# Attention logits of two pairs of steps in one visit of TensorE

## The chip, the cores and the metric

The kernel runs on one core of a Trainium2 chip. The metric is the device time in microseconds of one execution. Before the change it is 630.37 us (median of 3 runs, 630.08 to 630.44).

## The reference

A decoder trunk of two layers on 256 tokens of width 1024, all in float32. Each layer is

```
h = h + Mixer(RMSNorm(h))
h = h + square(relu(RMSNorm(h) @ w1)) @ w2        # 1024 -> 4096 -> 1024
```

The mixer of layer a is dilated sliding-window attention with three groups of 8 heads (windows and dilations 128/1, 512/4, 2048/16), merged by their softmax denominators; that of layer b is causal attention with 16 heads (with 256 tokens there is one block, its own). Both normalise queries and keys per head of 64, add a relative-position bias per head and mask:

```
q, k = rmsnorm(q_head), rmsnorm(k_head)
p = softmax(q @ k.T / 8 + bias + mask)            # float32, stable
o = p @ v ; Mixer = concat(o) @ w_o
```

## The kernel before, in words

All weights stream from HBM through one sequence of units of 256 rows x 512 columns. ScalarE rounds each 128-row slice to a high half (`next_hi`, L158) and VectorE makes the low half (`next_lo`, L173, instructions of L177 and L179); a dense product is then three matmuls per step (`mm3`, L231 to L233, and L654 to L656 in the MLP). The splits run several slices ahead of TensorE.

The order of the work is written out by hand. Every engine runs its instructions in the order in which the program issues them. After each `mm3` of a projection `beat()` (L211) counts one beat, issues what is due by then (`defer(beats, fn)`, L207; equal due times in the order in which they were deferred), and every second beat one more slice of the splits. So a due time is a place between the dense matmuls of TensorE, and at the same time a place in the queues of the other engines.

Attention is cut into 16 steps a layer, taken in pairs `m` (steps 2m and 2m+1, the two heads of a 128-row pair). In layer a a step is 128 query rows of one head position and four blocks of 128 keys; in layer b it is a whole head, three blocks. For a pair the stages are:

- `logits` (L505): 8 (layer b: 6) small matmuls a step, 16 or 12 a visit, on half the rows of the array each, into two PSUM banks of the tag `s`.
- `softmax` (L522) defers three things: one beat later `biased` (L536, VectorE: add the bias, L537, and take row maxima, L539), three beats later `exps` (L543, ScalarE, L545), five beats later `normed` (L547, VectorE: reciprocal, L550, and scaling, L552). They work in a buffer `L` of the pool, of which there are three.
- `turn` (L558): one step's probabilities are transposed on TensorE (L563) into a bank of the tag `tp`; a beat later ScalarE copies them out (`keep`, L567).
- `weigh` (L570): probabilities times values into a bank of the tag `o`, then `finish` (L587) splits the sums.

In `logits` a step counts matmuls as 4 (or 3) blocks, so a pair's visit has 8 matmuls in layer a and 6 in layer b as program statements, each run as two instructions in the trace (x16, x12).

`place` (L704) gives the due times: `logit_at`, `turn_at` and `weigh_at` per pair, counted from the start of the layer's projection. `project` has 16 beats for each of its entries (9 in layer a, 6 in layer b). Between them also stand the norms of the query and key heads: for an entry that ends at beat e, `head_norm` (L457) has GpSimd's power at e+4, the scaling of the two tiles of heads on VectorE at e+10 and e+11 (`normed`, L467), and their transposes on TensorE at e+13 and e+14 (`turned`, L472), also into banks `tp`, of which there are two. The entries of layer a with heads end at beats 16, 32, 48, 64, 80 and 96.

PSUM has eight banks: two each of `s`, `o`, `tp` and `acc`. The banks `o` hold nothing in a projection until the first `weigh`, due at beat 133 in layer a and 82 in layer b. A bias buffer is loaded for two head pairs ahead, by SP's queue, after the last `biased` of the pair before.

Of the kernel before, what the change touches and what calls it, by code (L numbers as in the profile page):

```python
# [67 lines left out]
def trunk(ctx, tc, x, rel_bias, norm_mix, norm_ffn, a_w_qkv, a_q_gain, a_k_gain, a_w_o,  # L68
          b_w_qkv, b_q_gain, b_k_gain, b_w_o, ffn_w1, ffn_w2, onehot, mask_a, mask_b, out):
    nc = tc.nc  # L70
# [12 lines left out]
    def bank(tag, name):  # L83
        return ps.tile([P, 512], F32, tag=tag, bufs=2, name=name)

    def work(tag, bufs, name):
        return act.tile([P, 512], F32, tag=tag, bufs=bufs, name=name)
# [119 lines left out]
    def defer(beats, fn):  # L207
        st["seq"] += 1
        later.append((st["beat"] + beats, st["seq"], fn))
# [279 lines left out]
    def attend(layer):  # L489


        npair = 4 if layer == "a" else 8
        steps = [(p, a, t) for p in range(npair) for t in range(NT) for a in range(2)] if layer == "a" else \
            [(p, a, None) for p in range(npair) for a in range(2)]
        nst = len(steps) // npair
        bias, probs, turned, o = {}, {}, {}, {}

        def blocks(a, t):

            if layer == "b":  # L500
                return [(1, None, 0), (1, None, 1), (0, None, 0)]
            own = [(t, g, t) for g in range(NG)]
            return own + [(0, 0, 1)] if t == 0 else [(1, 0, 0)] + own

        def logits(first):  # L505

            todo = []
            for n in (first, first + 1):
                p, a, t = steps[n]
                sp = bank("s", f"s_{layer}_{n}")  # L510
                rows = slice(a * HD, (a + 1) * HD)
                c, pr = p // 4, p % 4
                for i, (qt, g, kt) in enumerate(blocks(a, t)):
                    if layer == "a":
                        c, pr = g, p
                    todo.append((i, a, sp[:, i * P:(i + 1) * P], T["q"][rows, c, pr, qt * P:(qt + 1) * P],
                                 T["k"][rows, c, pr, kt * P:(kt + 1) * P]))
                softmax(n, sp)
            for _, _, dst, q, k in sorted(todo, key=lambda e: e[:2]):
                nc.tensor.matmul(dst, lhsT=q, rhs=k, start=True, stop=True)  # L520

        def softmax(n, sp):  # L522
            p, a, t = steps[n]
            L = work("L", 3, f"L_{layer}_{n}")
            bl = blocks(a, t)
            w = len(bl) * P
            nmax = small.tile([P, NT], F32, tag="nmax", name=f"nmax_{layer}_{n}")
            den = small.tile([P, NT], F32, tag="den", name=f"den_{layer}_{n}")
            off = P if layer == "a" and t == 0 else 0
            rows_of = []  # L530
            for qt in range(NT):
                mine = [i for i in range(len(bl)) if bl[i][0] == qt]
                if mine:
                    rows_of.append((qt, L[:, mine[0] * P:(mine[-1] + 1) * P]))

            def biased():  # L536
                nc.vector.tensor_add(L[:, :w], sp[:, :w], bias[p][:, a, off:off + w])  # L537
                for qt, lv in rows_of:
                    nc.vector.tensor_reduce(nmax[:, qt:qt + 1], lv, op=ALU.max, axis=AX.X, negate=True)  # L539
                if n % nst == nst - 1 and p + 2 < npair:  # L540
                    bias[p + 2] = load_bias(layer, p + 2)

            def exps():  # L543
                for qt, lv in rows_of:
                    nc.scalar.activation(lv, lv, AF.Exp, bias=nmax[:, qt:qt + 1], accum_out=den[:, qt:qt + 1])  # L545

            def normed():  # L547
                q0, q1 = rows_of[0][0], rows_of[-1][0]
                d = den[:, min(q0, q1):max(q0, q1) + 1]
                nc.vector.reciprocal(d, d)  # L550
                for qt, lv in rows_of:
                    nc.vector.tensor_scalar(lv, lv, den[:, qt:qt + 1], None, op0=ALU.mult)  # L552
            defer(1, biased)
            defer(3, exps)
            defer(5, normed)
            probs[n] = L

        def turn(n):  # L558
            p, a, t = steps[n]
            w = len(blocks(a, t)) * P  # L560
            tp = bank("tp", f"pt_{layer}_{n}")
            for i in range(w // P):
                nc.tensor.transpose(out=tp[:, i * P:(i + 1) * P], in_=probs[n][:, i * P:(i + 1) * P], identity=rev)  # L563
            pT = turned[n] = work("pT", NPT, f"pT_{layer}_{n}")

            def keep():
                nc.scalar.activation(pT[:, :w], tp[:, :w], AF.Copy)  # L567
            defer(1, keep)

        def weigh(first):  # L570

            todo = []
            for n in (first, first + 1):
                p, a, t = steps[n]
                if n % nst == 0:
                    o[p] = bank("o", f"o_{layer}_{p}")
                bl = blocks(a, t)
                col = ((p % 4) * 2 + a) * HD
                for i, (qt, g, kt) in enumerate(bl):
                    v = V[g if layer == "a" else p // 4]  # L580
                    todo.append((i, a, o[p][a * HD:(a + 1) * HD, qt * P:(qt + 1) * P], v[:, kt, col:col + HD],
                                 turned[n][:, i * P:(i + 1) * P], i == 0 or bl[i - 1][0] != qt,
                                 i == len(bl) - 1 or bl[i + 1][0] != qt))
            for _, _, dst, v, pt, start, stop in sorted(todo, key=lambda e: e[:2]):
                nc.tensor.matmul(dst, lhsT=v, rhs=pt, start=start, stop=stop)  # L585

        def finish(p):  # L587

            if p % 4 == 0:
                oT[p // 4] = tuple(act.tile([P, 4, S], F32R, tag="ol", bufs=4, name=f"o{s}_{layer}_{p}") for s in "hl")  # L590
            hi, lo = (z[:, p % 4, :] for z in oT[p // 4])
            i = o[p][:, 0:S]
            if layer == "b":
                hi, lo = (z.rearrange("p (b t q) -> p t q b", b=2, t=2) for z in (hi, lo))
                i = i.rearrange("p (t q b) -> p t q b", t=2, b=2)
            nc.scalar.activation(hi, i, AF.Copy)
            nc.vector.tensor_sub(lo, i, hi.bitcast(F32))

        def first_bias():
            for p in range(2):  # L600
                bias[p] = load_bias(layer, p)

        return first_bias, logits, turn, weigh, finish

    def wo_group(layer, n, acc, hc, ks, nhc, by_tile=False):
# [96 lines left out]
    defer(16, bias_vectors)  # L702

    def place(layer, logit_at, turn_at, weigh_at):  # L704
        first_bias, logits, turn, weigh, finish = attend(layer)
        nst = 4 if layer == "a" else 2
        defer(30 if layer == "a" else 2, first_bias)
        for n in range(16):
            m = n // 2
            defer(turn_at(m) + n % 2 * 3, lambda n=n: turn(n))  # L710
            if n % 2 == 0:
                defer(logit_at(m), lambda n=n: logits(n))
                defer(weigh_at(m), lambda n=n: weigh(n))
            if n % nst == nst - 1:
                defer(weigh_at(m) + 1, lambda n=n: finish(n // nst))


    place("a", lambda m: 64 + 14 * m if m < 4 else (112, 119, 126, 132.5)[m - 4],
          lambda m: 73 + 14 * m if m < 4 else 120 + 7 * (m - 4),
          lambda m: (133, 133, 133, 133, 146, 146, 150, 150)[m])  # L720
    project("a", order_a)
    acc = {0: [bank("acc", f"wo_a_0_{t}") for t in range(NT)]}
    wo_group("a", 0, acc[0], 0, [0, 1], 1, True)
# [10 lines left out]
    def to_second(n, y):  # L734
        add_half(n, y, rstd)
        norm_half(2, n, natural=True, lead=3)

    ffn(0, to_second)
    place("b", lambda m: 48 + 8 * m if m < 4 else (81.5, 87.5, 94, 100.5)[m - 4],
          lambda m: 57 + 8 * m if m < 4 else 90 + 6 * (m - 4),  # L740
          lambda m: (82, 82, 88, 88, 101, 101, 113, 113)[m])
    project("b", order_b)
    acc = {0: [bank("acc", f"wo_b_0_{t}") for t in range(NT)]}
    wo_group("b", 0, acc[0], 0, range(4), 2, True)
# [49 lines left out]
```

## Time and profile before

| | |
|---|---|
| time, median of 3 runs | 630.37 us |
| profiled execution | 630.4 us |
| its span, first to last instruction | 628.6 us |
| TensorE busy | 623.0 us (99%) |
| VectorE busy | 426.8 us (68%) |
| ScalarE busy | 385.1 us (61%) |
| GpSimd busy | 36.6 us (6%) |
| DMA, mean | 181 GB/s |

The span is split by engine: an engine is busy when an instruction of it runs. TensorE's matmuls are pipelined, so their durations overlap, and the distance from one start to the next says more than a duration. The granted clock of TensorE was full in every stretch of the page. Layer a's projection with its attention fills the first 137 us, layer b's lies between 332 and 417 us; in both stretches VectorE is busy for most of the time, although it is not over the whole span.

### The profile page before, as it was taken

Reading aid. Unit: us, or ns where it says so; the run is one execution under the profiler, and the core shown is the slowest. Engines: PE = TensorE matmul, PEld = TensorE weight load, DVE = VectorE, ACT = ScalarE, POOL = GpSimd, SP = SyncE. Lnnn points to the kernel's source line nnn. Section 1 sums busy time; section 2 is a strip of 40 time slices with the busy share of each in tenths; the row PEclk is TensorE's granted clock in tenths of the full one; section 3 lists DMA queues with packets and bytes.
Section 4 is the critical chain, followed back from the end, with each engine's and each line's share of the span. In section 5 each row is a group of like instructions: output and inputs, shape, how many; then the busy total and the mean of one; then the engine's idle time right before and its main releaser. Section 6 shows DMA issues by size and latency. Waiting matters only on the chain.

```text
span 628.6 us, 10380 instructions
## 1 busy us (share of the span) xinstructions
PE 623.0 (99%) x3902; PEld 541.2 (86%) x3902; DVE 426.8 (68%) x767; ACT 385.1 (61%) x742; POOL 36.6 (6%) x23
## 2 busy tenths in 40 slices
PE   8999999999999999999999999999999999999997
PEld 7778887888989989998988878778998899899886
DVE  5877988856875476467547789887776745754651
ACT  6866876765765356456537868777665644663540
POOL 1222221000000000000000332000000000000000
PEclk9999999999999999999999999999999999999999
DMA  7977456433655563574556657563467446645801
GB/s 250 315 196 241 124 187 174 163 108 124 215 174 190 205 223 140 187 254 140 174 179 202 196 180 195 142 186 125 157 211 260 147 161 230 220 127 191 250 18 68
DMA packets 74539, 113.62 MB, mean 181 GB/s; under 512 B 4585, under 2 KB 30505, under 8 KB 74489
## 3 DMA queue, kind: packets, MB, share of 16 engines
q1 hardware_dynamic: 74312, 112.82, 55.7%
q8 instruction: 31, 0.51, 0.3%
q14 instruction: 20, 0.16, 0.1%
q10 hardware_dynamic: 176, 0.14, 0.1%
HBM read 111.81 MB, written 1.13 MB: 180 GB/s over the span
## 4 chain that ended last, share of the span: by engine, by line
PE 97%; DVE 1%; DMA 1%; ACT 0%; issue 0%; DVEq 0%; SPq 0%; ACTq 0%
PE up L654 10%; PE up L656 9%; PE up L655 9%; PE y L231 9%; PE y L233 9%; PE y L232 9%; PE acc_a L231 6%; PE acc_a L232 5%; PE acc_a L233 5%; PE acc_b L231 3%; PE acc_b L233 3%; PE acc_b L232 3%; PE s_a L520 1%; PE o_a L585 1%; PE ut L355 1%; PE wo_b L231 1%
## 5 line engine op out<-in xcount | busy, mean ns | idle before, releaser
L179 DVE SCALAR_TENSOR_TENSOR lo<-raw,gt,hi 128x512 fp32r<-128x512 f32 x248 | 174.6, 745 | 7.4 <-ACT hi L169 7.2
L169 ACT ACTIVATE hi<-raw,gt 128x512 fp32r<-128x512 f32 x248 | 163.0, 714 | 5.7 <-PE y L233 2.8
L654 PE MATMUL up<-uh,hi 128*128 128x256 f32 x512 | 143.6, 281 | 0.0
L655 PE MATMUL up<-ul,hi 128*128 128x256 f32 x512 | 143.3, 280 | 0.0
L656 PE MATMUL up<-uh,lo 128*128 128x256 f32 x512 | 143.3, 280 | 0.0
L177 DVE TENSOR_TENSOR lo<-raw,hi 128x512 fp32r<-128x512 f32 x152 | 98.0, 685 | 42.0 <-ACT hi L167 41.8
L167 ACT ACTIVATE hi<-raw 128x512 fp32r<-128x512 f32 x152 | 88.1, 624 | 52.6 <-PE up L655 20.2
L231 PE MATMUL y<-hi,hh 128*128 128x512 f32 x256 | 99.8, 390 | 0.0
L233 PE MATMUL y<-hi,hl 128*128 128x512 f32 x256 | 99.6, 389 | 0.0
L232 PE MATMUL y<-lo,hh 128*128 128x512 f32 x256 | 99.6, 389 | 0.0
L656 PEld LDWEIGHTS up<-uh,lo 128*128 128x128 f32 x512 | 97.8, 191 | 0.0
L655 PEld LDWEIGHTS up<-ul,hi 128*128 128x128 f32 x512 | 96.1, 188 | 0.6
L654 PEld LDWEIGHTS up<-uh,hi 128*128 128x128 f32 x512 | 96.1, 188 | 0.5
L640 DVE TENSOR_TENSOR r<-r 128x512 f32<-128x512 f32 (+1 forms) x36 | 22.7, 631 | 65.6 <-ACT r L638 65.6
L638 ACT ACTIVATE r<-up 128x512 f32<-128x512 f32 (+1 forms) x36 | 19.8, 550 | 72.8 <-PE up L656 72.4
L231 PE MATMUL acc_a<-hi,uh 128*128 128x512 f32 x144 | 60.6, 421 | 0.0
L232 PE MATMUL acc_a<-lo,uh 128*128 128x512 f32 x144 | 57.0, 396 | 0.0
L233 PE MATMUL acc_a<-hi,ul 128*128 128x512 f32 x144 | 56.9, 395 | 0.0
L233 PEld LDWEIGHTS y<-hi,hl 128*128 128x128 f32 x256 | 48.0, 188 | 10.0
L231 PEld LDWEIGHTS y<-hi,hh 128*128 128x128 f32 x256 | 48.1, 188 | 9.4
L232 PEld LDWEIGHTS y<-lo,hh 128*128 128x128 f32 x256 | 48.1, 188 | 9.4
L231 PE MATMUL acc_b<-hi,uh 128*128 128x512 f32 x96 | 40.1, 418 | 0.0
(128 smaller groups left out, 777.4 us busy)
## 6 DMA issues: line engine op xcount, KB each, us to landing
raw<-in_ffn_w_dram SPq DMA_DIRECT2D x128, 512.0 KB, 4.9
raw<-in_a_w_qkv_dram SPq DMA_DIRECT2D x64, 256.0 KB, 4.3
raw<-in_b_w_qkv_dram SPq DMA_DIRECT2D x24, 512.0 KB, 4.6
raw<-in_b_w_o_dram SPq DMA_DIRECT2D x8, 512.0 KB, 5.0
bias_a<-vdram_a SPq DMA_DIRECT2D x20, 128.0 KB, 6.0
raw<-in_a_w_qkv_dram SPq DMA_DIRECT2D x4, 512.0 KB, 6.6
raw<-in_a_w_o_dram SPq DMA_DIRECT2D x4, 512.0 KB
bias_b<-vdram_b SPq DMA_DIRECT2D x8, 256.0 KB, 4.5
```

Of the source, the lines that this page charges most:

```text
L167: nc.scalar.activation(hi, w, AF.Copy)
L169: nc.scalar.activation(hi, w, AF.Copy, scale=gt[:, gain + c:gain + c + 1])
L177: nc.vector.tensor_sub(lo, w, hi.bitcast(F32))
L179: nc.vector.scalar_tensor_tensor(lo, w, gt[:, gain + c:gain + c + 1], hi.bitcast(F32), op0=ALU.mult, op1=ALU.subtract)
L231: nc.tensor.matmul(acc, lhsT=a[0], rhs=b[0], start=first, stop=False)
L232: nc.tensor.matmul(acc, lhsT=a[0], rhs=b[1], start=False, stop=False)
L233: nc.tensor.matmul(acc, lhsT=a[1], rhs=b[0], start=False, stop=last)
L638: defer(1, lambda: nc.scalar.activation(r, banks[b][:, :w], AF.Relu))
L640: defer(3, lambda: nc.vector.tensor_mul(r, r, r))
L654: nc.tensor.matmul(o, lhsT=whi[:, cols], rhs=uh, start=k == 0, stop=False)
L655: nc.tensor.matmul(o, lhsT=whi[:, cols], rhs=ul, start=False, stop=False)
L656: nc.tensor.matmul(o, lhsT=wlo[:, cols], rhs=uh, start=False, stop=k == 7)
```

## The change

Pairs get due times in tables. The logits of two neighbouring pairs may now have one due time; then the second pair is computed into the two banks `o` instead of `s`. In layer a this holds for all four twos of pairs, in layer b for the first four pairs. `turn` of the two steps of a pair is 2 beats apart instead of 3. There are four buffers `L` instead of three; the scratch that the program reserves for DMAs issued by GpSimd is cut to 8192 bytes.

```diff
-        def logits(first):
+        def logits(first, tag):
...
-                sp = bank("s", f"s_{layer}_{n}")
+                sp = bank(tag, f"s_{layer}_{n}")
...
-            L = work("L", 3, f"L_{layer}_{n}")
+            L = work("L", 4, f"L_{layer}_{n}")
...
-            defer(turn_at(m) + n % 2 * 3, lambda n=n: turn(n))
+            defer(turn_at[m] + n % 2 * 2, lambda n=n: turn(n))
             if n % 2 == 0:
-                defer(logit_at(m), lambda n=n: logits(n))
-                defer(weigh_at(m), lambda n=n: weigh(n))
+                tag = "o" if m and logit_at[m] == logit_at[m - 1] else "s"
+                defer(logit_at[m], lambda n=n, tag=tag: logits(n, tag))
+                defer(weigh_at[m], lambda n=n: weigh(n))
...
-    place("a", lambda m: 64 + 14 * m if m < 4 else (112, 119, 126, 132.5)[m - 4],
-          lambda m: 73 + 14 * m if m < 4 else 120 + 7 * (m - 4),
-          lambda m: (133, 133, 133, 133, 146, 146, 150, 150)[m])
+    place("a", (64, 64, 84, 84, 112, 112, 126, 126),
+          (73, 77, 93, 97, 121, 125, 135, 139),
+          (133, 133, 133, 133, 146, 146, 150, 150))
...
-    place("b", lambda m: 48 + 8 * m if m < 4 else (81.5, 87.5, 94, 100.5)[m - 4],
-          lambda m: 57 + 8 * m if m < 4 else 90 + 6 * (m - 4),
-          lambda m: (82, 82, 88, 88, 101, 101, 113, 113)[m])
+    place("b", (48, 48, 64, 64, 81.5, 87.5, 94, 100.5),
+          (57, 61, 73, 77, 90, 96, 102, 108),
+          (82, 82, 88, 88, 101, 101, 113, 113))
...
-    nc = _bacc.Bacc("TRN2", target_bir_lowering=False, num_devices=1)
+    nc = _bacc.Bacc("TRN2", target_bir_lowering=False, num_devices=1, dynamic_dma_scratch_size=8192)
```

## Rows read from the trace of the kernel before

**Rows 1.** The page, section 1: busy us (share of the span), instructions.
```profile
PE 623.0 (99%) x3902; PEld 541.2 (86%) x3902; DVE 426.8 (68%) x767; ACT 385.1 (61%) x742; POOL 36.6 (6%) x23
```

**Rows 2.** All waits of TensorE: waiter, releaser, us, times, longest.
```profile
PE warm_ps L261 <- DVE idle L255: 1.1, 1, 1.1
PE ut L355 <- DMA h<-in_x_dram: 0.6, 1, 0.6
```

**Rows 3.** Timeline of TensorE, layer a's first logits: start, us, operation.
```profile
57.99 0.39 PE L231 MATMUL acc_a<-hi,uh 128*128 128x512 f32 x1
...
58.45 0.39 PE L233 MATMUL acc_a<-hi,ul 128*128 128x512 f32 x1
58.77 1.16 PE L520 MATMUL s_a<-kT_a,qT_a 64*128 64x128 f32 x16
59.86 0.51 PE L231 MATMUL acc_a<-hi,uh 128*128 128x512 f32 x1
60.20 0.40 PE L232 MATMUL acc_a<-lo,uh 128*128 128x512 f32 x1
```

**Rows 4.** Timeline of TensorE, layer b's first logits and first `turn`.
```profile
368.89 0.94 PE L520 MATMUL s_b<-kT_b,qT_b 64*128 64x128 f32 x12
369.76 0.50 PE L231 MATMUL acc_b<-hi,uh 128*128 128x512 f32 x1
...
377.14 0.49 PE L563 MATMUL pt_b<-rev,L_b 128*128 128x128 f32 x3
```

**Rows 5.** TensorE around logits with 64 weighing matmuls, then 32 alone.
```profile
123.03 0.40 PE L233 MATMUL acc_a<-hi,ul 128*128 128x512 f32 x1
...
128.43 0.39 PE L232 MATMUL acc_a<-lo,uh 128*128 128x512 f32 x1
...
138.70 0.40 PE L233 MATMUL wo_a<-hi,ol_a 128*128 128x512 f32 x1
...
141.26 0.40 PE L232 MATMUL wo_a<-lo,oh_a 128*128 128x512 f32 x1
```

**Rows 6.** Timeline of VectorE after layer a's first logits; idle time before in brackets.
```profile
59.96 0.69 DVE L537 TENSOR_TENSOR L_a<-s_a,bias_a 128x512 f32<-128x512 f32 x1 [0.87 <-PE s_a L520]
...
62.61 0.74 DVE L179 SCALAR_TENSOR_TENSOR lo<-raw,gt,hi 128x512 fp32r<-128x512 f32 x1
...
64.73 0.16 DVE L550 RECIPROCAL den_a<-den_a 128x1 f32<-128x1 f32 x1
...
65.92 1.41 DVE L179 SCALAR_TENSOR_TENSOR lo<-raw,gt,hi 128x512 fp32r<-128x512 f32 x2
```

**Rows 7.** Timeline of TensorE, layer a's first `turn`.
```profile
66.17 0.60 PE L563 MATMUL pt_a<-rev,L_a 128*128 128x128 f32 x4
```

**Rows 8.** Timeline of VectorE from beat 84 to the scaling of heads.
```profile
78.21 2.07 DVE L179 SCALAR_TENSOR_TENSOR lo<-raw,gt,hi 128x512 fp32r<-128x512 f32 x3
81.75 0.69 DVE L467 TENSOR_TENSOR z_a<-z_a,r_a 128x512 f32<-128x512 f32 x1 [1.47 <-POOL r_a L463]
```

**Rows 9.** Timeline of VectorE after layer b's first logits.
```profile
369.86 0.56 DVE L537 TENSOR_TENSOR L_b<-s_b,bias_b 128x384 f32<-128x384 f32 x1 [0.66 <-PE s_b L520]
...
372.09 0.74 DVE L179 SCALAR_TENSOR_TENSOR lo<-raw,gt,hi 128x512 fp32r<-128x512 f32 x1
...
374.21 0.16 DVE L550 RECIPROCAL den_b<-den_b 128x2 f32<-128x2 f32 x1
...
375.53 0.74 DVE L179 SCALAR_TENSOR_TENSOR lo<-raw,gt,hi 128x512 fp32r<-128x512 f32 x1
```

**Rows 10.** A low half made on VectorE, and its first use on TensorE.
```profile
89.19 0.74 DVE L179 SCALAR_TENSOR_TENSOR lo<-raw,gt,hi 128x512 fp32r<-128x512 f32 x1
...
93.60 0.39 PE L232 MATMUL acc_a<-lo,uh 128*128 128x512 f32 x1
```

**Rows 11.** Groups of ScalarE: shapes, count, busy us, mean ns, idle before.
```profile
L545 ACT ACTIVATE L_a<-L_a,nmax_a 128x512 f32<-128x512 f32 x16 | 11.5, 722 | 7.5 <-DVE nmax_a L539 7.5
L567 ACT ACTIVATE pT_a<-pt_a 128x512 f32<-128x512 f32 x16 | 9.5, 593 | 5.7 <-PE pt_a L563 5.7
```

More of the change, by code (lines that the diff above doesn't have):

```diff
@@ L709, in place @@
             m = n // 2
-            defer(turn_at(m) + n % 2 * 3, lambda n=n: turn(n))
+            defer(turn_at[m] + n % 2 * 2, lambda n=n: turn(n))
             if n % 2 == 0:
-                defer(logit_at(m), lambda n=n: logits(n))
-                defer(weigh_at(m), lambda n=n: weigh(n))
+                tag = "o" if m and logit_at[m] == logit_at[m - 1] else "s"
+                defer(logit_at[m], lambda n=n, tag=tag: logits(n, tag))
+                defer(weigh_at[m], lambda n=n: weigh(n))
             if n % nst == nst - 1:
-                defer(weigh_at(m) + 1, lambda n=n: finish(n // nst))
-    place("a", lambda m: 64 + 14 * m if m < 4 else (112, 119, 126, 132.5)[m - 4],
-          lambda m: 73 + 14 * m if m < 4 else 120 + 7 * (m - 4),
-          lambda m: (133, 133, 133, 133, 146, 146, 150, 150)[m])
+                defer(weigh_at[m] + 1, lambda n=n: finish(n // nst))
+    place("a", (64, 64, 84, 84, 112, 112, 126, 126),
+          (73, 77, 93, 97, 121, 125, 135, 139),
+          (133, 133, 133, 133, 146, 146, 150, 150))
     project("a", order_a)
```

## The prediction

> **What bounds the kernel now.** I read the page's busy table first: TensorE is busy in 623.0 of 628.6 us [rows 1]. Then its waits: the longest is 1.1 us, at the very start [rows 2]. So TensorE never stands still in the middle of the program, and the time is the sum of what it issues. Two things can change that sum: less time per visit of small matmuls, or a wait where there was none. For the first I read TensorE's timeline around such visits, for the second VectorE's timeline in the same stretches, because VectorE makes what TensorE's later visits read.
>
> The profiled execution took 630.4 us (span 628.6, 1.8 around it); the median of the three runs is 630.37, so sums made on the one hold for the other.
>
> **What the change saves.** Two dense matmuls start 0.46 us apart over two steps, 57.99 to 58.45, so a plain step is 0.23 and a beat of three is 0.69 [rows 3]. From the last dense start before a visit of logits (58.45) to the second dense start behind it (60.20) are 1.75 us; two plain steps would be 0.46, so the visit costs 1.29 [rows 3]. From its first matmul to the next dense one a visit of 16 (8 pairs) takes 1.09 us, one of 12 (6 pairs) 0.87 [rows 3, 4]: 0.11 a pair. Of the 1.29, 8 x 0.11 = 0.88 is the pairs and 0.41 is getting in and out. That part is paid once less whenever two visits become one. Layer a goes from eight visits to four, layer b from eight to six: 6 x 0.41 = 2.46 us.
>
> One such saving existed already and is lost: the last logits of layer a (due at 132.5) ran directly ahead of the weighing due at 133. Logits and 64 weighing matmuls joined cost 128.43 - 123.03 - 0.46 = 4.94; 32 weighing matmuls alone cost 141.26 - 138.70 - 0.46 = 2.10, 64 would be 2.10 + 16 x 0.11 = 3.86, and with 1.29 for the logits 5.15 [rows 3, 5]. So 0.21 is lost, as the new due time 126 touches nothing. In layer b the visits due at 81.5, 87.5 and 100.5 keep their weighings. Net saving: 2.46 - 0.21 = 2.25 us.
>
> The Trainium skill, TensorEngine Tiling (Array Packing), section Tiling Modes, says that changing the tiling mode, not just the tile, drains TensorE. The rows agree in kind (0.41 a visit); if drains were all that mattered, the sum would be this 2.25 us alone, which is the first rival below.
>
> Transposes need no saving: `turn` at distances of 2 beats instead of 3 stays as many visits.
>
> **What the change adds: bursts on VectorE.** `biased` of all four steps is now queued at one beat, ahead of the four `normed`, and `turn` of the first step comes 9 beats behind the logits. VectorE works in order, so the first step's `normed` stands behind the other pair's `biased`. I count each merge from T, the start of its first logits matmul.
>
> TensorE's side in layer a: the first visit ends at T+1.09, the second pair adds 8 x 0.11 = 0.90, then come 9 beats (6.2) plus the slow first step. Before, the first `turn` of the pair due at 64 began at 66.17 = T+7.40 [rows 3, 7]; with the second pair T+8.30.
>
> VectorE's side, at 64: the first add starts at T+1.19 (59.96), held until then by the logits; a pair of adds and maxima takes 62.61 - 59.96 = 2.65 [rows 6]. Two pairs end at T+6.49. Between them and `normed` stand a split, the head sums and another split, 64.73 - 62.61 = 2.12, and a step's `normed` is (65.92 - 64.73) / 2 = 0.60 [rows 6]. First probabilities ready: T+9.21, against T+8.30. **Wait 0.9 us.** Later ones are in time: `turn` of the next steps follows every 1.8 us, `normed` every 0.6. The head transposes due at 77 and 78 stand behind two more `turn`, and by the same count find their inputs ready some 0.4 us before.
>
> At 84, in the middle of the heads of group 2: between the bursts stand two splits of 0.66 (three took 2.07 [rows 8]), so `normed` of the first step ends at 1.19 + 5.30 + 1.33 + 0.60 = T+8.42; `turn` at 93 wants it at T+8.30: wait 0.1. But the head transposes are due at 93 as well, directly behind it: a visit of four transposes is 0.60 - 0.27 + 0.11 = 0.44 [rows 7], so they want their input at T+8.86. That input is scaled at beat 90, behind all four `normed` of beat 89: 1.19 + 5.30 + 1.33 + 2.40 = T+10.22, plus 0.69 for the scaling itself [rows 8]: T+10.91. **Wait 2.0 us.** Before, VectorE stood idle 1.47 us ahead of this same scaling, waiting for GpSimd [rows 8]; that slack is what the burst eats, and more. The second tile (a split and a scaling later, 1.35) meets its transposes about 1.2 us later: wait 0.1.
>
> At 112 the stage has no head norms: two splits in between, T+8.42 against T+8.30: wait 0.1. At 126 the weighing due at 133, near 3.9 us of TensorE, lies between logits and `turn` at 135: no wait. That weighing needs the two borrowed banks back; they are free when the last add ends, near T+5.9, and TensorE comes there after 7 beats at T+7.3.
>
> Layer b, at 48 and 64: before, the first `turn` began at 377.14 = 368.89 + 8.25 [rows 4]; the visit due at 56 goes (1.07 by 6 pairs and 0.41) and six pairs come in (0.66): T+7.84. VectorE starts at T+0.97, two pairs take 2 x 2.23, then 2.12, then 0.66 [rows 9]: T+8.21. Wait 0.4 each, 0.8 in all. The head transposes at 61 and 62 come out even (both near T+12.1).
>
> Sum of waits: 0.9 + 2.0 + 0.3 + 0.8 = 4.0 us. Net: 4.0 - 2.25 = +1.75, and each wait has a short way from VectorE to TensorE that I left out, so a little more: 630.4 + 1.8 = **632.2 us**.
>
> The Trainium skill, TensorE: Matmul & The Clock Gate, in its opening table, lets TensorE pull weight loads ahead of running matmuls, and in "What overlaps and what doesn't" says that matmuls themselves start and end in program order. So dense matmuls queued behind a waiting transpose would not slip past; if they did, the waits would cost nothing.
>
> **Costed at nothing.** The exponentials: 0.72 us a step on ScalarE [rows 11], while VectorE hands it a step every 1.32; they keep up. Were they late, at most 0.7 us a merge. The weight splits: in layer a's logits the narrowest margin I found is a low half that ends at 89.94 and is read at 93.60, 3.66 us [rows 10]; in the changed order it is queued some beats after the burst of 84 has drained. If that cover fails, a wait of up to 1.6 us (the burst's 5.30 less 3.66). Bias loads are queued on SP up to 22 beats earlier and wait there for the adds; weight loads behind them are asked for by splits that stand behind the same adds on VectorE, so nothing new waits. The fourth buffer of probabilities and the smaller scratch only move memory; GpSimd issues no DMA here.
>
> One cost the trace does not show. At beats 77/78 and 93/94 (layer a), 61/62 and 77/78 (layer b) three transposing visits fall on two beats with two `tp` banks, so the third waits until ScalarE has emptied the first. ScalarE has about 1.6 us for a copy of 0.59 [rows 11]; I take nothing, and up to 0.6 a place, 2.4 in all, as the upper end. Below nothing it can't go, as it only adds a wait.
>
> **Rivals.** (1) Faster: the bursts don't reach TensorE, and only the visits count: 630.4 - 2.25 = 628.2. For it: not one wait in the middle of the program before, and 1.47 us of VectorE idle at the place of the largest wait. Against: at 64 the old margin was 7.40 - (1.19 + 2.65 + 2.12 + 0.60) = 0.84 us, and the burst adds 2.65 to VectorE's side and 0.90 to TensorE's. So the old margin would have to be 1.75 us for this case. (2) A draw: the wait of 2.0 at beat 93 stays out (its scaling ahead of `normed` after all, or VectorE further ahead), the small ones come: 630.4 - 2.25 + 2.0 = 630.2. (3) Much slower: the `tp` banks come late as well, 632.2 + 2.4 = 634.6. (4) The change doesn't do what it says: something keeps the two visits apart, so that no 0.41 is saved and the waits still come: 632.2 + 2.46 = 634.7. Against it: both are due on one beat and leave the queue one after the other, and the borrowed banks are idle then.
>
> **Chances.** Forecast (631.2 to 633.6) 0.58; rival 1 0.18; rival 2 0.14; rivals 3 and 4 together 0.10. The range 629.3 to 634.5 leaves out rival 1 and most of 3 and 4; the forecast's own is 631.2 to 633.6. A measurement tells 0.2% (1.3 us) from no change: faster, under 629.1, 0.17; same 0.18; slower, over 631.6, 0.65.
>
> **What would show it.** In the changed trace: 16 + 16 logits in one run of about 2.0 us to the next dense start, four times in layer a and twice (12 + 12) in b. TensorE waits that were not there: about 0.9 us before `turn` near 67 us, released by VectorE's L552 (scaling of probabilities); about 2.0 before the head transposes of L472 near 86 to 90 us, released by L467; 0.4 at the first `turn` behind each merge of layer b. TensorE idle in all near 6 us instead of 1.7. The prediction is wrong if these waits are missing (then the time is near 628), or if waits appear on ScalarE's copies of L567 or on splits.

## The result and the profile after

The changed kernel takes 635.6 us (median of 4 runs, 633.89 to 636.48), the kernel before, run beside it, 630.23: a ratio of 1.0078 [1.0065, 1.0091]. It is slower, as forecast, but by 5.4 us and not by 1.8, and 635.6 lies above the range of 629.3 to 634.5. In a later set it took 634.21 against 630.49, 1.0062 [1.0049, 1.0074]. The profiled execution took 636.23 us (span 634.4), 5.8 us more than that of before (630.4). Of the four executions the one at 633.89 has a mean granted clock of 0.999, the other three 0.997; only the one at 636.23 left a trace.

The page of the changed kernel, section 1, answers to [rows 1]:

```profile
PE 624.9 (98%) x3902; PEld 542.5 (86%) x3902; DVE 427.5 (67%) x767; ACT 386.6 (61%) x742; POOL 36.2 (6%) x23
```

As many instructions as before on every engine, and busy times nearly as before. What is new is idle time of TensorE. All its waits in the changed kernel, against the two of [rows 2]:

```profile
PE t_a L472 <- DVE z_a L467: 1.8, 1, 1.8
PE pt_a L563 <- DVE den_a L550: 1.1, 2, 1.0
PE warm_ps L261 <- DVE idle L255: 1.1, 1, 1.1
PE pt_b L563 <- DVE den_b L550: 0.9, 2, 0.4
PE ut L355 <- DMA h<-in_x_dram: 0.8, 1, 0.8
```

The head transposes wait for the scaling of heads, and the first `turn` behind a merge waits for the scaling of probabilities, in both layers. (The list names L550 there: it is the next step's reciprocal, which VectorE starts just as that scaling, L552, ends.) The other two waits stood there before.

TensorE's timeline around the first merged visit and the first `turn` behind it:

```profile
59.48 0.39 PE L233 MATMUL acc_a<-hi,ul 128*128 128x512 f32 x1
59.80 2.06 PE L520 MATMUL s_a<-kT_a,qT_a 64*128 64x128 f32 x32
61.78 0.51 PE L231 MATMUL acc_a<-hi,uh 128*128 128x512 f32 x1
62.12 0.40 PE L232 MATMUL acc_a<-lo,uh 128*128 128x512 f32 x1
...
67.86 0.40 PE L233 MATMUL acc_a<-hi,ul 128*128 128x512 f32 x1
69.22 0.63 PE L563 MATMUL pt_a<-rev,L_a 128*128 128x128 f32 x4 [0.97 <-DVE den_a L550]
```

The two visits did become one (x32). It costs 62.12 - 59.48 - 0.46 = 2.18 us; two single ones cost 2 x 1.29 = 2.58 [rows 3]. So 0.40 is saved here, and 0.41 was forecast. Then `turn` starts 1.36 behind the last dense matmul instead of 0.23: 1.13 us are lost, of which the row shows 0.97 as idle. (A dense matmul lasts 0.40 but hands over after 0.23; idle time is counted from its end.)

VectorE's timeline in the changed kernel, first behind the merge at beat 64, then behind that at 84:

```profile
60.99 0.69 DVE L537 TENSOR_TENSOR L_a<-s_a,bias_a 128x512 f32<-128x512 f32 x1 [0.88 <-PE s_a L520]
...
65.67 0.69 DVE L539 TENSOR_REDUCE nmax_a<-L_a 128x1 f32<-128x512 f32 x1
...
68.59 0.48 DVE L552 TENSOR_SCALAR L_a<-L_a,den_a 128x512 f32<-128x512 f32 x1
...
89.74 0.69 DVE L467 TENSOR_TENSOR z_a<-z_a,r_a 128x512 f32<-128x512 f32 x1
```

Four additions and maxima in a row (60.99 to 66.28), and the first scaled probabilities at 68.59 + 0.48 = 69.07; TensorE starts 0.15 later. In the second stretch the heads are scaled by 90.43, with no idle time ahead, where before VectorE had stood idle 1.47 us [rows 8].

TensorE behind the merge at 84:

```profile
87.62 0.40 PE L233 MATMUL acc_a<-hi,ul 128*128 128x512 f32 x1
88.19 0.63 PE L563 MATMUL pt_a<-rev,L_a 128*128 128x128 f32 x4 [0.17 <-DVE den_a L550]
90.57 0.41 PE L472 MATMUL t_a<-rev,z_a 128*128 128x128 f32 x2 [1.75 <-DVE z_a L467]
...
91.53 0.63 PE L232 MATMUL acc_a<-lo,uh 128*128 128x512 f32 x1
91.96 0.63 PE L233 MATMUL acc_a<-hi,ul 128*128 128x512 f32 x1
```

The wait of 1.75 is there. Behind it stands what no step of the prediction had: two dense steps lie 91.96 - 91.53 = 0.43 apart, where a plain step is 0.23 [rows 3]. The same stretch in windows of 1 us (busy us and instructions of PE, PEld, DVE, ACT and POOL, then the granted clock, DMA share, GB/s):

```profile
90.00:91.00 1.00, 0.43 (x5) 0.46 (x5) 1.00 (x2) 0.53 (x2) 0.00 (x0) 0.98 0.62 108
91.00:92.00 1.00, 1.00 (x5) 0.81 (x4) 1.00 (x3) 0.66 (x2) 0.00 (x0) 0.50 0.89 246
...
94.00:95.00 1.00, 1.00 (x7) 0.76 (x6) 1.00 (x2) 0.00 (x0) 0.00 (x0) 0.81 0.74 137
95.00:96.00 1.00, 1.00 (x6) 0.82 (x5) 0.07 (x1) 0.91 (x2) 0.00 (x0) 1.00 0.96 371
```

The granted clock is half from shortly before 91.0 until 94.4: 0.02 + 3.00 x 0.5 + 0.19 = 1.7 us of full-speed work are lost.

Layer b, TensorE's merged visit and the `turn` behind it, against [rows 4]:

```profile
373.83 1.61 PE L520 MATMUL s_b<-kT_b,qT_b 64*128 64x128 f32 x24
382.27 0.52 PE L563 MATMUL pt_b<-rev,L_b 128*128 128x128 f32 x3 [0.43 <-DVE den_b L550]
```

One difference has nothing to do with the change. The first logits come 1.03 us later than before (59.80 against 58.77 [rows 3]), and the whole of it arises before 13 us. TensorE's timeline at the start, first of the kernel before, then of the changed one:

```profile
9.93 0.63 PE L232 MATMUL acc_a<-lo,uh 128*128 128x512 f32 x1
10.36 0.44 PE L233 MATMUL acc_a<-hi,ul 128*128 128x512 f32 x1
10.64 0.40 PE L231 MATMUL acc_a<-hi,uh 128*128 128x512 f32 x1
```

```profile
11.43 0.63 PE L232 MATMUL acc_a<-lo,uh 128*128 128x512 f32 x1
11.86 0.63 PE L233 MATMUL acc_a<-hi,ul 128*128 128x512 f32 x1
12.28 0.48 PE L231 MATMUL acc_a<-hi,uh 128*128 128x512 f32 x1
```

Steps 0.43 apart end near 10.4 us in one execution and near 12.3 in the other. The traces of the runs below show that this differs from execution to execution: their first logits start between 58.39 and 59.97 us. The granted clock reads 1.00 from 8 to 12 us in both executions here, although the steps lie as far apart as those at 0.50 above; in `late_heads` and `filled` the same stretch reads 0.57. So a reading of 1.00 is no proof of full speed at the start, and what slows these steps down here stays open.

The account of the two profiled executions, between the same dense matmuls of each: +1.04 before the first logits, +3.96 in layer a from there on, +0.84 in layer b; sum 5.84, and 636.23 - 630.4 = 5.8.

### The profile page after: what moved, and what is told of

The parts are those of the page before. It is cut to its first block, busy times and chain, and to the rows that moved or that the text cites. A ratio compares the mean times of both kernels' runs of the same rounds, so it can differ in the third digit from the quotient of the medians.

```text
span 634.4 us, 10371 instructions
## 1 busy us (share of the span) xinstructions
PE 624.9 (98%) x3902; PEld 542.5 (86%) x3902; DVE 427.5 (67%) x767; ACT 386.6 (61%) x742; POOL 36.2 (6%) x23
## 3 DMA queue, kind: packets, MB, share of 16 engines
HBM read 111.81 MB, written 1.13 MB: 178 GB/s over the span
## 4 chain that ended last, share of the span: by engine, by line
PE 92%; DVE 6%; DMA 1%; issue 1%; DVEq 0%
PE up L654 9%; PE up L655 9%; PE up L656 9%; PE y L232 9%; PE y L233 9%; PE y L231 9%; PE acc_a L231 5%; PE acc_a L232 4%; PE acc_a L233 4%; PE acc_b L231 3%; PE acc_b L233 3%; PE acc_b L232 3%; PE ut L355 1%; PE wo_b L231 1%; DVE L_a L537 1%; PE o_a L585 1%
```

## The experiments

The theory after the result: the visits save what was forecast; VectorE's bursts cost more than that in waits; and in the profiled execution TensorE's clock fell behind the longest of them. The rivals: the other layout of memory costs something; the third user of two `tp` banks is late; the fall of the clock is a chance that has nothing to do with the wait.

**The parts alone.** `a_only`, the change in layer a alone; layer b has its old times:

```diff
-    place("b", (48, 48, 64, 64, 81.5, 87.5, 94, 100.5),
-          (57, 61, 73, 77, 90, 96, 102, 108),
+    place("b", (48, 56, 64, 72, 81.5, 87.5, 94, 100.5),
+          (57, 65, 73, 81, 90, 96, 102, 108),
```

> Layer a has the due times of the change, layer b those of before (turns 3 beats apart). My theory (each merge saves one way in and out, and VectorE's burst makes TensorE wait; the longest wait is followed by a stretch at half clock): waits of about 1.0 before the first turn of the merge at 64, 0.2 and 1.8 at the merge at 84, 0.1 at 112, and a half-clock stretch of 3.4 us behind the 1.8, in all about +4 us on the kernel before: 634.3. Rival (the cost lies in the start or in the memory layout, not in attention): 631 to 632, and no change of the shift along layer a.

Measured: 633.99 us (633.1 to 634.96), 1.0055 [1.0041, 1.0068]. TensorE's waits in it that the kernel before has not:

```profile
PE t_a L472 <- DVE z_a L467: 1.8, 1, 1.8
PE pt_a L563 <- DVE den_a L550: 1.1, 2, 1.0
...
PE pt_a L563 <- DVE kT_a L479: 0.2, 1, 0.2
```

(Left out is one of 0.3 us for a low half at 10.65 us, long before the first merge.) The expected half clock did not come: in its profiled execution (633.1) the clock stayed full behind the wait. Late starts of TensorE in layer a took 4.24 us there, counted from start to start, and the visits gave back 1.39; net +2.85. The last of the three waits is not in the list of the changed kernel above, where TensorE was slowed down and came too late to meet it, but it is in that of `after_again`, the same kernel at full clock. It is a wait for a `tp` bank. L479 is VectorE's copy of the transposed keys out of such a bank, and the second `turn` behind the merge at 84 (due at beat 95) wants the bank next. VectorE and TensorE in `a_only`:

```profile
91.74 0.42 DVE L479 COPY kT_a<-t_a 128x256 f32<-128x256 f32 x1
```

```profile
92.21 0.66 PE L563 MATMUL pt_a<-rev,L_a 128*128 128x128 f32 x4 [0.17 <-DVE kT_a L479]
```

The copy ends at 92.16 and the `turn` starts at 92.21, 0.56 behind the last dense start (91.65) instead of 0.23: 0.33 us are lost. No run has the change with its second `turn` 3 beats behind the first, so what the 2 beats add to this wait is not shown.

`b_only`, the change in layer b alone (layer a with the due times of before):

> Layer b has the due times of the change, layer a those of before. My theory: two merges save 0.8 us, two waits of 0.6 before the first turn of each come in, no half clock: between 630.5 and 631.3. Rival by the prediction's own count (waits of 0.4): 630.2. Rival that the banks of the sums cost something by themselves: above 631.5 with waits elsewhere than at the turns.

Measured: 631.42 us (630.95 to 632.63, 11 runs), 1.0017 [1.0008, 1.0026], 0.1 above the expected stretch; the waits are the two before `turn` in layer b, as expected. The two parts make +0.55% and +0.17%, together 0.72%; the whole change makes 0.78% and 0.62% in its two sets. Within their intervals they add up.

`memory_only`, the due times of before in both layers, with the fourth buffer and the smaller scratch:

> All due times are those of before; only the fourth buffer of probabilities and the smaller scratch of the change stay. The changed run was already 1.0 us late before its first logits. If the layout of memory or the scratch causes that, this kernel takes 631.2 or more. If it is chance of one run (when the full clock comes at the start), it takes 630.2 like before.

Measured: 630.15 us (629.72 to 631.33, 11 runs), 0.9996 [0.9987, 1.0005]. The layout costs nothing, and so the late start in the profile above is not its doing.

**The merge without the burst.** `spread` merges visits, but the second pair's `softmax` is deferred to the due time at which it stood before (`late` beats behind the visit); the `turn` keep their old times. Merged are the pairs at 64 and at 92 in layer a, and at 48 and 64 in layer b:

```diff
-                softmax(n, sp)
+                if late:
+                    defer(late, lambda n=n, sp=sp: softmax(n, sp))
+                else:
+                    softmax(n, sp)
...
+    place("a", (64, 64, 92, 92, 112, 119, 126, 132.5),
+          (73, 87, 101, 115, 120, 127, 134, 141),
+          (133, 133, 133, 133, 146, 146, 150, 150),
+          (64, 78, 92, 106, 112, 119, 126, 132.5), 3)
```

> Logits of two pairs in one visit at 64 and 92 of layer a and at 48 and 64 of layer b, the second pair in the banks of the sums, but everything behind the logits at the due times of before: the second pair's adds, maxima, exponentials and scalings 14 (layer a) or 8 (layer b) beats after its logits, turns as before. My theory: four ways in and out are saved and no burst stands before a turn: 630.2 - 4 x 0.4 = 628.6, no new waits. Rival that a merged visit itself costs as much as two: 630.2.

Measured: 629.23 us (628.91 to 630.07, 11 runs), 0.998 [0.9971, 0.9989]: 1.3 us faster than before (630.54 beside it), where 1.6 were expected. All waits of TensorE's matmuls in it, over the whole program:

```profile
PE warm_ps L261 <- DVE idle L255: 1.1, 1, 1.1
PE ut L355 <- DMA h<-in_x_dram: 0.5, 1, 0.5
```

The list is that of before. Each merge saved 0.35 to 0.42 in the trace; 0.40 went again at the logits of 112. TensorE reached them 0.7 us earlier than in the kernel before, while VectorE still copied the keys, and their row lasts 1.56 us instead of 1.16:

```profile
101.60 1.56 PE L523 MATMUL s_a<-kT_a,qT_a 64*128 64x128 f32 x16
```

(The weight loads inside that visit wait; the list counts only matmuls.) So merging pays by itself; the change loses by when the work behind the visits is done.

**Is it the order on VectorE alone?** `order_only` keeps the change's due times, but puts the second pair's `softmax` 5 beats later (not at the last merge of layer a), behind the first pair's scaling:

```diff
+                late = 5 if tag == "o" and (layer, m) != ("a", 7) else 0
+                defer(logit_at[m], lambda n=n, tag=tag, late=late: logits(n, tag, late))
```

> The changed kernel with its visits, banks and turns, but the second pair's adds, maxima, exponentials and scalings 5 beats later, so that VectorE has the first pair's scalings ahead of the second pair's adds (not at the last merge of layer a). My theory that the order on VectorE makes the waits: the waits before the first turns go (1.0, 0.2 and 0.1 in layer a, two of 0.45 in layer b), the one of 1.8 before the first head transpose at 93 becomes about 1.2 before the second, some 0.5 may come before the second pair's turns; 630.5 to 632.0. Rival that the borrowed banks or the turns 2 beats apart cost the time: like the changed kernel, over 634.

Measured: 636.95 us (635.41 to 637.54), 1.0094 [1.0078, 1.011]: slower than the change itself, so this expectation failed. Two of its waits of TensorE, and the place of the longest, on TensorE and on ScalarE:

```profile
PE t_a L472 <- ACT pT_a L570: 2.1, 2, 1.7
...
PE pt_a L566 <- ACT pT_a L570: 1.0, 1, 1.0
```

```profile
87.88 0.60 PE L566 MATMUL pt_a<-rev,L_a 128*128 128x128 f32 x4
...
91.26 0.44 PE L472 MATMUL t_a<-rev,z_a 128*128 128x128 f32 x2 [1.65 <-ACT pT_a L570]
```

```profile
87.98 0.73 ACT L548 ACTIVATE L_a<-L_a,nmax_a 128x512 f32<-128x512 f32 x1 [1.15 <-DVE nmax_a L542]
...
89.30 0.72 ACT L548 ACTIVATE L_a<-L_a,nmax_a 128x512 f32<-128x512 f32 x1 [0.51 <-DVE nmax_a L542]
...
90.63 0.57 ACT L570 ACTIVATE pT_a<-pt_a 128x512 f32<-128x512 f32 x1
```

The first `turn` is in time now (87.88), but its copy out of the `tp` bank runs only at 90.63: ScalarE works in order, and ahead of the copy stand two exponentials that wait for VectorE's maxima, now late. The next head transposes need that bank. So here the prediction's third rival, late `tp` banks, is the longest wait. Neither of the two orders tried serves all the stages of four steps that lie close together here; with fewer merges and the work spread out, as in the run before, they fit.

Part of the time is the clock again. Behind the wait of 1.65 and, three dense steps later, one of 0.75 before another `turn` (93.36) the granted clock is half:

```profile
94.00:96.00 2.00, 2.00 (x8) 1.61 (x7) 1.20 (x3) 1.41 (x3) 0.00 (x0) 0.50 0.93 301
```

The one execution with a mean granted clock of 1.0 took 635.41 us. It too is slower than those of the changed kernel beside it with 0.999 (634.06 to 634.21), so by that one execution the order itself costs near 1.2 us more than the change's, and not 2.7.

`late_heads` takes the longest wait from the other end: the changed kernel with the head transposes of that one entry 3 beats later.

```diff
-            defer(13 + t, lambda t=t: turned(t))
+            defer((16 if nm == "a4" else 13) + t, lambda t=t: turned(t))
```

> The changed kernel, but the two head transposes due at 93 and 94 (the wait of 1.8) come 3 beats later, at 96 and 97; VectorE's order stays. My theory: that wait goes, and with it the clock's fall, so 634.2 - 1.9 = 632.3 in all executions. Rival that VectorE as a whole is late: the wait turns up at the next thing that reads from VectorE, and the time stays above 634.

Measured: 633.97 us (633.29 to 634.18), 1.0052 [1.0039, 1.0064], beside 634.21 of the changed kernel on the same chip. Expected were some 2 us less. In the list of TensorE's waits the longest has another releaser and is 1.5 us instead of 1.8:

```profile
PE t_a L472 <- ACT pT_a L567: 1.5, 1, 1.5
```

Again the `tp` banks: moved, the head transposes stand between other `turn`, and the second tile waits for a copy of ScalarE. The medians hide that a part of the gain came: between the same dense matmuls the profiled execution loses 0.8 us less in layer a than that of `after_again`, but it was 0.65 us later at the first logits (59.27 against 58.62).

**The clock.** `after_again` is the changed kernel once more, to see how often the clock falls:

> The changed kernel itself once more, as the measure for the other runs of this chip. My theory: 3.8 us above before where the clock stays up behind the wait of 1.8, some 1.7 more where it falls to half for 3.4 us, so times in two groups near 634.2 and 636, and a lower mean clock in the second. Rival (one fixed cost): one group.

Measured: 634.21 us (634.06 to 635.28). Three executions lie at 634.06 to 634.21 with a mean granted clock of 0.999, the others at 634.67 (0.997) and 635.28 (0.996); a second group near 636 did not come, and half clock at the start can lower the mean as well, so the two theories stay undecided here. In its profiled execution the same wait of 1.8 us stands in the list, and the granted clock stays full behind it. The windows from 88 to 96 us (columns as above):

```profile
88.00:92.00 4.00, 2.59 (x14) 1.75 (x14) 3.96 (x9) 2.92 (x6) 0.00 (x0) 1.00 0.70 182
92.00:96.00 4.00, 3.83 (x22) 3.22 (x23) 3.17 (x6) 3.10 (x6) 0.00 (x0) 1.00 0.72 214
```

The same kernel with the same wait: half clock for 3.4 us in one execution, none in another. `filled` tried to take the cause away: 8 matmuls of 128x128 on constants between the `turn` of beat 93 and the head transposes, with their result unused, so that TensorE works while it would wait.

```diff
+            if layer == "a" and n == 4:
+                dummy = bank("s", "dummy")
+                for i in range(8):
+                    nc.tensor.matmul(dummy[:, 0:P], lhsT=rev, rhs=rev, start=True, stop=True)
```

> The changed kernel, but between the first turn of beat 93 and the head transposes that wait there TensorE runs eight extra matmuls of 128x128 on constants (about 1.7 us) into a free bank; their result is not used. The wait of 1.8 shrinks to near nothing, the time to that point does not change. My theory that the wait costs its own length and, in some executions, the clock behind it: no execution loses clock there, time near 634.2 in all of them, 1.2 to 1.5 below the changed kernel's median. Rival that the clock falls for another reason: times like the changed kernel's, in two groups.

Measured: 634.61 us (634.31 to 634.83), 1.0063 [1.0051, 1.0076]. All five runs lie within 0.5 us, where the nine of the changed kernel lie between 633.89 and 636.48. But the median is no better than that of `after_again` beside it, three of whose five runs have a mean granted clock of 0.999; the profiled execution of `filled` was 0.74 us later at the first logits (59.36 against 58.62). Inconclusive. So the wait was made longer, once with and once without work in it. `longer_wait` puts four VectorE multiplications of 128x512, unused, ahead of that scaling; `filled_long` is the same with 18 constant matmuls in the wait:

```diff
+            if nm == "a4" and t == 0:
+                junk = work("junk", 2, "spare")
+                for i in range(4):
+                    nc.vector.tensor_mul(junk, zs[1], zs[1])
```

> The changed kernel with four more VectorE multiplications of 128x512 into a spare tile ahead of the scaling of heads that TensorE waited 1.8 us for at beat 93; their result is used nowhere. The wait grows by about 4 x 0.69 = 2.8 us to 4.6. Theory (TensorE's clock falls to half because of the wait at beat 93, and at 1.8 us it does so in some executions only): the fall comes in nearly all executions now and costs at least the 1.7 us it cost before: 634.3 + 2.8 + 1.7 = 638.8, and the profile shows the granted clock at half behind the wait. Rival (the fall is a chance of the execution that has nothing to do with the wait): 634.3 + 2.8 = 637.1, at most with a fall in some executions.

> The same longer wait, but TensorE runs 18 matmuls of 128x128 on constants, whose result is used nowhere, ahead of the waiting transposes, about 4.1 us of work: it arrives when its input is nearly ready. Theory (the clock falls because TensorE stood still): no fall here, 634.3 + 2.8 = 637.1, at most 0.3 more, so about 1.7 us less than the run with the longer wait and no matmuls in it. Rival (nothing to do with the wait): both the same within 0.3.

Measured: `longer_wait` 639.22 us (638.24 to 640.05), 1.0133 [1.0119, 1.0147]; `filled_long` 636.94 (636.81 to 637.36), 1.0099 [1.0084, 1.0115], 2.3 us less although TensorE does 18 matmuls more. TensorE's timeline, first of `longer_wait`, then of `filled_long`:

```profile
93.53 0.66 PE L476 MATMUL t_a<-rev,z_a 128*128 128x128 f32 x2 [4.54 <-DVE z_a L471]
...
94.85 0.63 PE L232 MATMUL acc_a<-lo,uh 128*128 128x512 f32 x1
95.27 0.63 PE L233 MATMUL acc_a<-hi,ul 128*128 128x512 f32 x1
```

```profile
92.11 0.44 PE L476 MATMUL t_a<-rev,z_a 128*128 128x128 f32 x2 [0.42 <-DVE z_a L471]
...
92.84 0.40 PE L232 MATMUL acc_a<-lo,uh 128*128 128x512 f32 x1
93.07 0.40 PE L233 MATMUL acc_a<-hi,ul 128*128 128x512 f32 x1
```

And the window from 92 to 96 us of `longer_wait`, then of `filled_long`, where the granted clock is the third number from the end:

```profile
92.00:96.00 4.00, 2.47 (x9) 2.10 (x10) 3.97 (x8) 1.08 (x2) 0.00 (x0) 0.50 0.37 139
```

```profile
92.00:96.00 4.00, 3.72 (x21) 2.71 (x22) 4.00 (x9) 1.91 (x4) 0.00 (x0) 1.00 0.15 31
```

Half clock and steps 0.42 apart behind the empty wait, full clock and steps 0.23 apart behind the filled one. Of the 3.2 us between these two executions 1.3 arose before the first logits (59.97 against 58.65) and 1.9 behind them. All four runs of `longer_wait` have a mean granted clock of 0.994 or less, all four of `filled_long` 0.997 or more. The rival expected both within 0.3 us of each other, and it falls: TensorE standing still for 4.5 us brought the clock down. That the shorter wait of 1.75 did the same in the changed kernel is inferred from this, not shown. The Trainium skill, TensorE: Matmul & The Clock Gate, Part 1 (What's actually happening), says that the clock is set by how busy TensorE has been recently; these two runs agree (0.50 against 1.00).

**A version that beats both.** `spread_more` is `spread` with one merge more: in layer a the logits are due at 64, 64, 92, 92, 113, 119, 119 and 132.5, each pair's `softmax` where it stood before (the one of 112 a beat later).

> The visits merged as in the run named spread (second pair's softmax later), but with a merge also at 119 (the pairs due at 112 and 119 before are at 113 and alone at 119 with the next one): five merged places instead of four, and the logits of the fifth pair of layer a one beat later, behind the copies of the keys that it waited 0.40 us for. Theory (visits are worth 0.35 to 0.42 us each when no softmax is moved ahead of its time): 629.2 less 0.4 for the visit less up to 0.4 for the wait, 628.3 to 628.8, no new wait of TensorE over 0.3 us. Rival (the exponentials and copies behind 119 have no room left for two pairs): a wait of about 0.5 to 1 us near the turns of 127 and 134, 629.2 or more.

Measured: 628.51 us (628.33 to 629.19), 0.9965 [0.9953, 0.9978], 2.4 us less than before; TensorE waits only at the start, as in the kernel before. Five visits saved at 0.41 are 2.05; between the same dense matmuls the profiled executions show 1.9 (1.15 in layer a, 0.77 in layer b), and the interval of the ratio is 1.4 to 3.0 us.

## Why the prediction was wrong

**What bounds the kernel, and the saving: right.** 2.25 us net were forecast; the traces show 1.39 in layer a (1.43 by the same sum) and 0.82 in layer b. The visits joined, so rival 4 is out. Borrowed banks, splits and memory cost nothing that the list of waits shows behind the start of the program.

**Which waits: right but for one, and VectorE's times nearly exact.** From the start of each merge, first scaled probabilities at 64 were forecast for T+9.21 and came at T+9.27; the scaled heads behind 84 for T+10.91, and came at T+10.86; layer b's for T+8.21, and came at T+8.29. On TensorE's side 8 x 0.11 is 0.88 and not the 0.90 written; the trace has 0.89 (1.98 less 1.09). Rival 1 fell because the waits came; so did rival 2, which had the one at beat 93 stay out. The idle time of the new waits sums to 1.8 + 1.1 + 0.9 = 3.8 us in the list, against 4.0.

**The sum that follows: too small, in three terms.** The step that failed is "each wait has a short way from VectorE to TensorE that I left out, so a little more: 630.4 + 1.8". First, that way is 0.15 us at the first late start (69.07 to 69.22), and TensorE is late at one more place in layer a than was counted, the `turn` that lost 0.33 us to a `tp` bank: the loss from start to start is 4.24 us in layer a where 3.2 was forecast, and 1.66 in layer b (0.84 net and 0.82 saved) where 0.8 was. (In layer b the two first `turn` lose 0.59 each, starting 0.82 behind the last dense matmul instead of 0.23; the rest are late starts of 0.1 to 0.2 that were not counted.) With 5.9 for waits instead of 4.0 the sum is 630.4 + 5.9 - 2.2 = 634.1, where `after_again` lies (634.21), and inside the range. Second, the prediction treated TensorE's time as the sum of its work and its waits, each step at full clock. A wait can also slow down what follows it: in the profiled execution 1.7 us were lost so, and 1.1 of it reached the time (layer a lost 3.96 net with the fall, 2.85 without), in part because a slower TensorE waited less: the wait of 0.2 is missing in its list. Third, that execution had 1.0 us from its start, which is chance. 3.7 + 1.1 + 1.0 = 5.8. So the first term is an error of the sum, near 1.9 us; that the median of 635.6 fell outside the range came with the other two, and for the three executions without a trace it is open which of them it was.

The runs don't show how often the clock falls at this wait; of the three profiled executions with the wait of 1.8 (the changed kernel twice, `a_only`), one has the fall. That of `order_only`, with 1.65 and 0.75, has one too; that of `late_heads`, with 1.46, has none.

**Costed at nothing: the `tp` banks did cost a little.** The prediction asked only whether ScalarE empties them in time, and no wait for ScalarE came; rival 3 with its 2.4 us did not either. But heads of keys are copied out by VectorE, the busy engine, and that copy held a `turn` up by 0.33 us in `a_only` and `after_again`. As soon as another order takes the longest wait on VectorE away, those banks become the next one, 1.65 us in `order_only` and 1.46 in `late_heads`. That they cost so little in the change was a coincidence of its order and no reserve.

## What to carry to other kernels

Merge the visits of an engine if each visit has a price, but do not let the work that follows them be issued in one burst: defer the consumers' work to where it was due before, and only the saving is left. Where a bound engine gets a new wait, count the way of the signal at every late start, not the idle time alone, and add what the clock may lose behind the wait. If a wait that you remove comes back with another releaser, look for a shared buffer behind it: moving one stage then wins less than the wait was long.

## What the hardware showed that was not expected

- TensorE's granted clock fell to half for 3.4 us behind a wait of 1.75 us in one execution and not in two others; behind 4.54 us it fell, and all four runs of that kernel took at least 0.88 us more than any of the one whose wait was filled with matmuls on constants. Before both falls TensorE had run one `turn` and then stood still.
- At the start dense steps stand 0.43 us apart until 10.4 us in one execution and until 12.3 in another, which makes 1.0 us of chance in a kernel of 630.
- Two PSUM banks shared by two kinds of transposes tie TensorE to the order of both engines that empty them: the same two banks held it up for VectorE's copy in one order (0.17 us idle) and for ScalarE's in two others (1.65 and 1.46).
- A dense matmul that lasts 0.40 us hands over after 0.23, so a late start costs 0.17 us more than the idle time that the trace shows for it.
